# Two-block mixer kernel on one core: z products first in the first SSD group, and sixteen modulation tiles moved out of SSD groups 2 and 3 into attention and merge

## Chip, cores and metric

One core of one Trainium2 chip runs the whole program as one launch. The metric is the time of one execution in device microseconds (us): the median of the runs shown.

## What is computed

512 tokens of 1024 dimensions, all in f32, go through a first block and a second one. What the change touches lies in the first block:

```
mod = silu(c) @ w_ada + b_ada                  # 6 x 1024 numbers
shift1, scale1, gate1, shift2, scale2, gate2 = split(mod, 6)
h = rms_norm(x, norm1_w) * (1 + scale1) + shift1
q, k, v, xBC, z, dt_raw, gates = split(h @ w_in)
attn = softmax attention(q, k, v)              # 16 heads, 4 kv heads
ssd  = ssd_mixer(xBC, z, dt_raw)               # conv, 4 groups, both directions, * silu(z), norm
merged = sigmoid(g_attn) * (attn @ w_attn_out) + sigmoid(g_ssd) * (ssd @ w_ssd_out)
x = x + gate1 * (merged @ w_o)
h2 = rms_norm(x, norm2_w) * (1 + scale2) + shift2
x = x + gate2 * (relu(h2 @ w_mlp1)**2 @ w_mlp2)
```

The second block (a gated linear recurrence, then latent attention, then a norm) is untouched.

## The kernel before

Every product is made from f32 operands split in a high and a low part, so each 128x128 by 128x512 step is three matmuls (`mm3`, printed in the profile as lines L174, L175 and L176). A GEMM with eight contraction tiles is thus 24 matmuls on TensorE (PE). Its 512 KB weight tile is loaded by `weight()`: an SP-issued DMA (L159) into a slot of the pool `wr`, a cast on ScalarE (ACT) to the high part `wh` (L162), and a subtraction for the low part `wl` (L165) on VectorE (DVE) or GpSimd (POOL). `wr`, `wh` and `wl` have four slots each, so weights run up to four GEMMs ahead of PE. PSUM for GEMMs is the pool `pm`, also four slots: the fifth GEMM waits until the first one's reader is done.

The order of the program text is turned into one queue per engine by a scheduler: it pulls ready work from later in the text forward, and each engine then runs its own queue strictly in order.

**Modulation.** `mod` has 48 columns of 128. `mod_tiles(j)` (L274) makes one: a 512 KB tile `wada` of `w_ada` is loaded by a DMA on SP into a slot of the same pool `wr`, and one DVE instruction (L279) multiplies it by silu(c) and sums along the row into column j of `modc`. Columns 0 to 15 are made in norm1. Columns 16 to 23 are gate1, 24 to 31 shift2, 32 to 39 scale2, 40 to 47 gate2. All of 16 to 47 get their bias in one DVE instruction after merge (L373), and are first used after that. So the time at which these 32 are made is free, and the table `MODS` spreads the first sixteen of them over SSD groups 2 and 3 (six and ten), eight go into attention (letters "m" of the table `ATT`), and the last eight into merge, one for each of its eight steps.

**The SSD mixer** (`ssd`, `ssd_core`, `ssd_out`). norm1 hands over seven finished products: dt and the six xBC tiles of group 0. For these the program does the first half of `dt_product` (softplus, ending with `av`, L465), then convolutions (`conv`: ACT L498, four DVE steps L507, tanh L515, DVE L516). The second half of `dt_product` (L471 to L490: decay sums on PE, copies, exponentials) stands before the fourth convolution. Then each group g runs its `ssd_core`: transposes to token-major (L561, L566), the product CB (L572) with two masked copies (DVE L576), and the 18 steps of the table `CORE`: six state steps S (DVE L596 scales, PE L598, DVE L603 and L604, PE L608, DVE L612, L613 or L615), eight mixer steps M for one head each (PE L623, then four times ACT L629, DVE L631, ACT L633, DVE L635, then ACT L642 and the POOL product L643), four outputs Y for two heads each (PE L650 and L653, DVE L657, L659, L670, POOL L666). Y0 follows M3, Y3 is last and needs the POOL products of M6 and M7.

Between those steps `ssd` spreads fills, GEMMs that keep PE busy: the z products of the same group (one DVE instruction L534 as reader, used by L659), the xBC products of the next group with their convolutions (six DVE instructions each with the reader), and `ssd_out` of the group before. In group 0 the fills alternate between xBC and z:

```
fill = so + [xs[0], zs[0], xs[1], zs[1], xs[2], zs[2], xs[3], zs[3], xs[4], xs[5]]
```

**Attention** (`attention`) overlaps the scores, the softmax (DVE L755, L759, ACT L758, POOL L763), transposes and products of 16 heads with the qkv products, the stacks of rotated q and k (DVE L820 to L823 and L170, PE L807), and gate products.

**Merge** (`merge`) has eight steps of two GEMMs: a gate product (weights `w_gate`), the attention output (`w_attn_out`) with DVE readers L921 and L922, and `mod_tiles([40 + m])`. Merge's early work is pulled forward into the end of attention by the scheduler. After it come the bias of `modc` (L373), `gate_rows` and the output projection.

Of the kernel before, what the change touches and what calls it, by code (L numbers as in the profile page):

```python
# [18 lines left out]
FIRST = [-1, 4, 5, 0, 1, 2, 3]  # L19
# [20 lines left out]
AORD = "s0 s1 s2 s3 f0 t0 m0 t1 m1 t2 m2 t3 m3 f1".split()  # L40
CORE = "S0 S1 M0 S2 S3 M1 S4 S5 M2 M3 Y0 M4 M5 Y1 M6 M7 Y2 Y3"
NC = 19
MODS = [0, 0, 6, 10]
WP = 0
TP = 0
LO = {"start": 5, "ssd": 8, "attn": 2, "merge": 3, "mlp": 0, "rglru": 3, "mla_in": 6, "mla": 5}
# [13 lines left out]
class Build:  # L60
# [616 lines left out]
    def ssd(self, first):  # L677
        nc, a = self.nc, self.a
        self.csb = self.c([128, 512], "csb", F32R)
        self.tk1 = self.c([128, 4, 128], "tk1")  # L680
        self.tk2 = self.c([128, 4, 128], "tk2")
        self.dcy = self.c([128, 4, 64], "dcy")
        self.ssacc = self.c([128, 512], "ssacc", pool=self.stack[-2]["c"])
        self.xb = [[None] * 6 for _ in range(4)]
        self.zt, self.ssdT = {}, {}
        for i, ps in zip(FIRST, first):
            if i < 0:
                dt = self.dt_product(ps)
                next(dt)
                continue  # L690
            if i == FIRST[4]:
                next(dt)
            with self.fills():
                self.xb[0][i] = self.conv(i if i < 4 else 16 + 4 * (i - 4), ps)
        with self.fills():
            for i in range(6):
                if i not in FIRST:
                    self.xbc(0, i)
        self.qk = {}
        for g in range(4):  # L700
            so = [lambda mp=mp: self.ssd_out(g - 1, mp) for mp in range(4)] if g else []
            zs = [lambda j=j: self.z(g, j) for j in range(4)]
            if g < 3:
                xs = [lambda i=i: self.xbc(g + 1, i) for i in (4, 5, 0, 1, 2, 3)]
                fill = so + [xs[0], zs[0], xs[1], zs[1], xs[2], zs[2], xs[3], zs[3], xs[4], xs[5]]
            else:
                with self.fills():
                    self.attn_tables(self.stack[-2]["c"])
                q0 = self.qkv(0)
                fill = so + zs + [lambda: next(q0, None)] * Q0  # L710
            k0 = 16 + sum(MODS[:g])
            k1 = k0 + MODS[g]
            fill = [lambda f=f, i=i: (f(), self.mod_tiles([k0 + i] if k0 + i < k1 else [])) for i, f in enumerate(fill)]
            n = 0
            for step, _ in enumerate(self.ssd_core(g)):
                while n < len(fill) and n * NC <= (step + 1) * len(fill):
                    with self.fills():
                        fill[n]()
                    n += 1
            while n < len(fill):  # L720
                with self.fills():
                    fill[n]()
                n += 1
        for mp in range(4):
            with self.fills():
                for _ in range(2):
                    next(q0, None)
            self.ssd_out(3, mp)
        with self.fills():
            for _ in q0:  # L730
                pass
        R = self.ssacc
        p = self.ps()
        nc.tensor.matmul(p, lhsT=self.ones, rhs=self.ssacc, start=True, stop=True)
        nc.scalar.activation(out=R, in_=p, func=AF.Sqrt, scale=1.0 / 2048, bias=self.eps)
        nc.vector.reciprocal(out=R, in_=R)
# [100 lines left out]
    def attention(self):  # L837
        nc = self.nc

        def scores(h, t):  # L840
            stk, (kh, kl), vv = self.qk[h // 4]
            p = self.ps()
            s = slice(t * 128, t * 128 + 128)
            nc.tensor.matmul(p, lhsT=stk[h % 4][:, s], rhs=kh, start=True, stop=False)
            nc.tensor.matmul(p, lhsT=stk[h % 4][:, s], rhs=kl, start=False, stop=True)
            return self.softmax_tile(p, 512)

        def turn(pr, kt):
            p = self.ps()
            for t in range(NT):  # L850
                nc.tensor.transpose(out=p[:, t * 128:t * 128 + 128], in_=pr[t][:, kt * 128:kt * 128 + 128],  # L851
                                    identity=self.ident)
            ph, pl = self.t("ph", F32R), self.t("pl", F32R)
            self.split(ph, pl, p)
            return ph, pl

        def mix(h, po, kt, parts):
            vv, (ph, pl) = self.qk[h // 4][2], parts
            nc.tensor.matmul(po, lhsT=vv[:, kt], rhs=ph, start=kt == 0, stop=False)
            nc.tensor.matmul(po, lhsT=vv[:, kt], rhs=pl, start=False, stop=kt == 3)  # L860

        def output(h, po):

            if h % 2 == 0:
                self.of = self.t("of")
            of = self.of
            d = slice(64 * (h % 2), 64 * (h % 2) + 64)
            e = slice(64 * (1 - h % 2), 64 * (1 - h % 2) + 64)
            nc.scalar.copy(out=of[d], in_=po[e])
            nc.vector.tensor_tensor(out=of[d], in0=of[d], in1=po[d], op=ALU.add)  # L870
            if h % 2 == 1:
                self.split(self.oh[:, h // 2], self.ol[:, h // 2], of)

        gates = [lambda m=m: self.gate_ssd(m) for m in range(8)]
        mods = list(range(16 + sum(MODS), 40))

        def fill(what):
            with self.fills():
                for x in what:
                    if x == "q":  # L880
                        next(nxt, None)
                    elif x == "g" and gates:
                        gates.pop(0)()
                    elif x == "m" and mods:
                        self.mod_tiles([mods.pop(0)])

        pr = [scores(0, t) for t in range(NT)]
        for h in range(16):
            g, i = divmod(h, 4)
            if i == 0:  # L890
                nxt = self.qkv(g + 1) if g < 3 else iter(())
            last = pr
            if i == 3:
                fill("q" * 8)
            pr = []
            po = self.pm() if POM else self.ps()
            turned = {}
            for x in AORD:
                j = int(x[1])
                if x[0] == "s" and h < 15:  # L900
                    pr.append(scores(h + 1, j))
                elif x[0] == "t":
                    turned[j] = turn(last, j)
                elif x[0] == "m":
                    mix(h, po, j, turned.pop(j))
                elif x[0] == "f":
                    fill(ATT[g][2 * i + j])
            output(h, po)
        fill("g" * 8 + "m" * len(mods))

    def merge(self):
        nc, a = self.nc, self.a
        oh, ol, acc, mh, ml = self.oh, self.ol, self.accS, self.mh, self.ml
        for m in range(8):
# [7 lines left out]
                self.split(mh[:, m], ml[:, m], th)  # L922

            self.gemm_cm([[a["w_attn_out"][m]]], lambda k: (oh[:, k], ol[:, k]), evac)
            self.mod_tiles([40 + m])

    def gate_rows(self, j, s):
        nc, a = self.nc, self.a
# [598 lines left out]
```

## Time and profile before

| | us |
|---|---|
| median of 3 runs | 1647.56 (1647.04 to 1647.98) |
| the profiled execution | 1645.17 |
| its span on the core | 1643.4 |
| PE busy in the span | 1579.3 (96%) |
| DVE busy | 1126.8 (69%) |
| ACT busy | 789.5 (48%) |
| POOL busy | 446.5 (27%) |

The mean granted clock of TensorE was 0.995 of full speed. How to read it: PE is busy nearly all the time, so what counts is the few places where PE has a gap, and which engine ends that gap. A busy share of 69% for DVE is an average over stages in which it is full and stages in which it is half empty. In the trace SSD group 0 runs from about 94 to 178 us, group 1's core begins there, the fills of groups 2 and 3 with their modulation tiles lie between 239 and 451 us, attention ends about 742 us, merge about 812 us.

### The profile page before, as it was taken

Reading aid. Unit: us, or ns where it says so; the run is one execution under the profiler, and the core shown is the slowest. Engines: PE = TensorE matmul, PEld = TensorE weight load, DVE = VectorE, ACT = ScalarE, POOL = GpSimd, SP = SyncE. Lnnn points to the kernel's source line nnn. Section 1 sums busy time; section 2 is a strip of 40 time slices with the busy share of each in tenths; the row PEclk is TensorE's granted clock in tenths of the full one; section 3 lists DMA queues with packets and bytes.
Section 4 is the critical chain, followed back from the end, with each engine's and each line's share of the span. In section 5 each row is a group of like instructions: output and inputs, shape, how many; then the busy total and the mean of one; then the engine's idle time right before and its main releaser. Section 6 shows DMA issues by size and latency. Waiting matters only on the chain.

```text
span 1643.4 us, 20885 instructions
## 1 busy us (share of the span) xinstructions
PE 1579.3 (96%) x7696; PEld 1279.9 (78%) x7696; DVE 1126.8 (69%) x1948; ACT 789.5 (48%) x1517; POOL 446.5 (27%) x322
## 2 busy tenths in 40 slices
PE   5989999999999999999999999999999999999998
PEld 3767677677688778778889888888888778988886
DVE  6899689689869988874454344343458884747873
ACT  4347546355465667663344232322337662455652
POOL 3414345254252344321133011111141011321012
PEclk9999999999999999999999999999999999999999
DMA  7511124224222222215323232323323222322211
GB/s 255 197 57 60 52 87 130 66 82 146 78 77 91 71 71 90 78 52 192 103 64 116 90 103 91 102 90 103 112 70 99 87 90 67 100 69 71 64 62 52
DMA packets 50648, 153.54 MB, mean 93 GB/s; under 512 B 8177, under 2 KB 12913, under 8 KB 50546
## 3 DMA queue, kind: packets, MB, share of 16 engines
q1 hardware_dynamic: 50546, 152.22, 28.9%
q8 instruction: 60, 0.98, 0.2%
q14 instruction: 42, 0.34, 0.1%
HBM read 150.10 MB, written 2.10 MB: 93 GB/s over the span
## 4 chain that ended last, share of the span: by engine, by line
PE 72%; DVE 16%; ACT 4%; issue 3%; POOL 3%; DMA 1%; SPq 0%; DVEq 0%; POOLq 0%; ACTq 0%
PE pm L174 19%; PE pm L175 19%; PE pm L176 19%; DVE acc L507 2%; PE px L608 1%; DVE wada L279 1%; DVE nmax L755 1%; DVE wl L165 1%; PE px L851 1%; PE px L598 1%; POOL rs L254 1%; DVE w L635 1%; PE px L860 1%; PE px L653 1%; PE px L650 1%
## 5 line engine op out<-in xcount | busy, mean ns | idle before, releaser
L162 ACT CAST wh<-wr 128x1024 fp32r<-128x1024 f32 (+5 forms) x245 | 239.5, 980 | 390.3 <-PE pm L175 176.0
L165 DVE TENSOR_TENSOR wl<-wr,wh 128x1024 fp32r<-128x1024 f32 (+2 forms) x170 | 201.6, 1187 | 182.3 <-ACT wh L162 181.6
L165 POOL TENSOR_TENSOR wl<-wr,wh 128x1024 fp32r<-128x1024 f32 (+3 forms) x75 | 175.9, 2347 | 530.6 <-ACT wh L162 483.3
L174 PE MATMUL pm<-hh,wh 128*128 128x512 f32 (+1 forms) x432 | 172.9, 404 | 7.9 <-ACT hh L169 6.2
L175 PE MATMUL pm<-hl,wh 128*128 128x512 f32 (+1 forms) x432 | 175.0, 405 | 3.4 <-POOL hl L170 3.4
L176 PE MATMUL pm<-hh,wl 128*128 128x512 f32 (+1 forms) x432 | 172.4, 399 | 0.0
L986 POOL TENSOR_TENSOR r<-r 128x512 f32<-128x512 f32 x32 | 50.9, 1589 | 252.3 <-ACT r L985 252.3
L174 PE MATMUL pm<-h,wh 128*128 128x512 f32 (+1 forms) x288 | 105.4, 366 | 0.0
L175 PE MATMUL pm<-h,wh 128*128 128x512 f32 (+1 forms) x288 | 105.2, 365 | 0.0
L176 PE MATMUL pm<-h,wl 128*128 128x512 f32 (+1 forms) x288 | 105.2, 365 | 0.0
L174 PEld LDWEIGHTS pm<-hh,wh 128*128 128x128 f32 (+1 forms) x432 | 81.2, 188 | 29.4 <-ACT hh L169 7.6
L175 PEld LDWEIGHTS pm<-hl,wh 128*128 128x128 f32 (+1 forms) x432 | 81.6, 189 | 26.1 <-POOL hl L170 6.3
L174 PE MATMUL pm<-wh,rh 128*128 128x512 f32 x256 | 99.8, 390 | 0.0
L763 POOL TENSOR_SCALAR pr<-pr,psum 128x512 f32<-128x512 f32 x64 | 64.6, 1021 | 129.1 <-DVE psum L759 71.1
L176 PE MATMUL pm<-wh,rl 128*128 128x512 f32 x256 | 99.6, 389 | 0.0
L175 PE MATMUL pm<-wl,rh 128*128 128x512 f32 x256 | 99.6, 389 | 0.0
L176 PEld LDWEIGHTS pm<-hh,wl 128*128 128x128 f32 (+1 forms) x432 | 81.5, 189 | 19.7 <-issue 3.1
L507 DVE SCALAR_TENSOR_TENSOR acc<-pm,conv_w_s,acc 128x510 f32<-128x510 f32 (+2 forms) x114 | 84.5, 741 | 9.0 <-ACT acc L498 8.0
L643 POOL TENSOR_TENSOR e<-e,w 128x512 f32<-128x512 f32 x32 | 52.0, 1625 | 100.5 <-ACT e L642 74.5
L279 DVE SCALAR_TENSOR_TENSOR wada<-wada,cs 128x1024 f32<-128x1024 f32 x48 | 66.3, 1390 | 15.6 <-DMA wada<-in_w_ada 15.3
L758 ACT ACTIVATE pr<-px,nmax 128x512 f32<-128x512 f32 (+2 forms) x96 | 60.4, 637 | 29.9 <-DVE nmax L755 24.0
L174 PE MATMUL pm<-ha,wh 128*128 128x512 f32 (+1 forms) x192 | 68.2, 355 | 0.0
(401 smaller groups left out, 4130.1 us busy)
## 6 DMA issues: line engine op xcount, KB each, us to landing
wr<-in_w_mlp SPq DMA_DIRECT2D x64, 512.0 KB, 3.4
wada<-in_w_ada SPq DMA_DIRECT2D x48, 512.0 KB, 3.9
wr<-in_w_xbc SPq DMA_DIRECT2D x24, 512.0 KB, 3.5
wr<-in_w_in_a SPq DMA_DIRECT2D x20, 512.0 KB, 3.5
wr<-in_w_z SPq DMA_DIRECT2D x16, 512.0 KB, 3.5
wr<-in_w_ssd_out SPq DMA_DIRECT2D x16, 512.0 KB, 3.5
wr<-in_w_gate SPq DMA_DIRECT2D x16, 512.0 KB, 4.0
wr<-in_w_qkv SPq DMA_DIRECT2D x16, 384.0 KB, 3.1
```

What stands on the lines that cost most here:

```text
L162: nc.scalar.copy(out=hi[:, :n], in_=raw[:, :n])
L165: eng.tensor_tensor(out=lo[:, :n], in0=raw[:, :n], in1=r32(hi[:, :n]), op=ALU.subtract)
L174: m(out, lhsT=lh, rhs=rh, start=start, stop=False)
L175: m(out, lhsT=lh, rhs=rl, start=False, stop=False)
L176: m(out, lhsT=ll, rhs=rh, start=False, stop=stop)
L254: g.tensor_tensor(out=r, in0=r, in1=self.mhalf.to_broadcast(list(ss.shape)) if len(ss.shape) == 2 else self.mhalf.unsqueeze(2).to_broadcas ...
L279: nc.vector.scalar_tensor_tensor(out=w, in0=w, scalar=1.0, in1=self.cs, op0=ALU.mult, op1=ALU.mult, accum_out=self.modc[:, j:j + 1])
L507: nc.vector.scalar_tensor_tensor(out=acc[:, lo:hi], in0=ps[:, lo + o:hi + o], scalar=w[:, j:j + 1], in1=acc[:, lo:hi], op0=ALU.mult, op1=A ...
L643: self.e("ew").tensor_tensor(out=e, in0=e, in1=w, op=ALU.mult)
L758: nc.scalar.activation(out=e[:, :n], in_=p, func=AF.Exp, bias=nmax, accum_out=s)
L763: self.e("norm").tensor_scalar(out=e[:, :n], in0=e[:, :n], scalar1=s, scalar2=1.0, op0=ALU.mult, op1=ALU.mult)
L986: self.e("sq").tensor_tensor(out=r, in0=r, in1=r, op=ALU.mult)
```

## The change

Three things change in the text; no operation is added or left out, only its place moves.

- `MODS` becomes all zero: SSD groups 2 and 3 make no modulation columns. Attention's eight are now columns 16 to 23 (before 32 to 39). Each of merge's eight steps makes three columns (24+m, 32+m, 40+m) where it made one. So sixteen tiles, with sixteen DMAs on SP and sixteen DVE instructions, move from the SSD groups to merge's text.
- In group 0, z(0,0) and z(0,1) stand before the second half of `dt_product`, and this stands after all six convolutions where it stood before the fourth one.
- Group 0's fills are now z(0,2), z(0,3) and then the six xBC products of group 1.

```diff
-MODS = [0, 0, 6, 10]
+MODS = [0, 0, 0, 0]
...
-            if i == FIRST[4]:
-                next(dt)
             with self.fills():
                 self.xb[0][i] = self.conv(i if i < 4 else 16 + 4 * (i - 4), ps)
         with self.fills():
             for i in range(6):
                 if i not in FIRST:
                     self.xbc(0, i)
+            self.z(0, 0)
+            self.z(0, 1)
+        next(dt)
...
-                fill = so + [xs[0], zs[0], xs[1], zs[1], xs[2], zs[2], xs[3], zs[3], xs[4], xs[5]]
+                fill = zs[2:] + xs if g == 0 else so + [xs[0], zs[0], xs[1], zs[1], xs[2], zs[2], xs[3], zs[3], xs[4], xs[5]]
...
-        mods = list(range(16 + sum(MODS), 40))
+        mods = list(range(16, 24))
...
-            self.mod_tiles([40 + m])
+            self.mod_tiles([24 + m, 32 + m, 40 + m])
```

What this does to the queues, at the three places of which the prediction speaks (line numbers of the changed kernel are one higher after line 690):

DVE at the start of group 0's core, before. `acc` is a convolution, `zt` a z product, `cb` and `xw` the first tiles of the core; the convolutions here read the first and third fill of group 1's xBC tiles from `pm`.

```order
108 L507 SCALAR_TENSOR_TENSOR acc_758<-pm_727,conv_w_s,acc_758 128x510
109 L507 SCALAR_TENSOR_TENSOR acc_758<-pm_727,conv_w_s,acc_758 128x511 x2
110 L576 TENSOR_TENSOR cb_772<-px_767,k_tri_s 128x512
111 L507 SCALAR_TENSOR_TENSOR acc_758<-pm_727,conv_w_s,acc_758 128x510
112 L576 TENSOR_TENSOR cb_774<-px_767,k_tri_s 128x512
113 L596 TENSOR_TENSOR xw_777<-xtm_695,tk_587 128x512
114 L516 SCALAR_TENSOR_TENSOR th_764<-th_764,acc_758 128x512
115 L534 SCALAR_TENSOR_TENSOR zt_817<-zt_817,pm_786 128x512
116 L596 TENSOR_TENSOR xw_820<-xtm_695,tk_587 128x512
```

The same place of DVE in the changed kernel:

```order
109 L534 SCALAR_TENSOR_TENSOR zt_705<-zt_705,pm_674 128x512
110 L534 SCALAR_TENSOR_TENSOR zt_739<-zt_739,pm_708 128x512
111 L576 TENSOR_TENSOR cb_834<-px_829,k_tri_s 128x512
112 L534 SCALAR_TENSOR_TENSOR zt_826<-zt_826,pm_795 128x512
113 L576 TENSOR_TENSOR cb_836<-px_829,k_tri_s 128x512
114 L596 TENSOR_TENSOR xw_839<-xtm_763,tk_587 128x512
115 L534 SCALAR_TENSOR_TENSOR zt_888<-zt_888,pm_857 128x512
116 L596 TENSOR_TENSOR xw_848<-xtm_763,tk_587 128x512
117 L615 TENSOR_TENSOR yoff_838<-px_845,tk_587 128x512
118 L615 TENSOR_TENSOR yoff_838<-px_854,tk_587 128x512
119 L596 TENSOR_TENSOR xw_915<-xtm_763,tk_587 128x512
120 L631 SCALAR_TENSOR_TENSOR e_895<-pf_891,tk_586,e_895 128x128
```

The first four GEMMs are now z products with one reader each, and the convolutions of group 1's tiles come later.

POOL at the end of group 0, before (`e` is the product of a mixer step, `ssacc` the sum of squares, `wl` a weight's low part):

```order
44 L666 TENSOR_TENSOR ssacc<-ssacc,sq_1276 128x512
45 L643 TENSOR_TENSOR e_1287<-e_1287,w_1288 128x512
46 L165 TENSOR_TENSOR wl_1657<-wr_1655,wh_1656 128x1024
47 L643 TENSOR_TENSOR e_1351<-e_1351,w_1352 128x512
48 L666 TENSOR_TENSOR ssacc<-ssacc,sq_1387 128x512
```

The same place of POOL in the changed kernel:

```order
43 L165 TENSOR_TENSOR wl_1657<-wr_1655,wh_1656 128x1024
44 L643 TENSOR_TENSOR e_1240<-e_1240,w_1241 128x512
45 L666 TENSOR_TENSOR ssacc<-ssacc,sq_1276 128x512
46 L643 TENSOR_TENSOR e_1327<-e_1327,w_1328 128x512
47 L643 TENSOR_TENSOR e_1351<-e_1351,w_1352 128x512
```

The low part `wl_1657` stood between the products of M6 and M7; now it stands ahead of M5's.

DVE in the last quarter of attention, before (`wada` is the first of merge's modulation tiles, `pl`, `st`, `m`, `nmax` and `psum` belong to attention):

```order
931 L759 RECIPROCAL psum_6053<-psum_6053 128x1
932 L279 SCALAR_TENSOR_TENSOR wada_6930,modc<-wada_6930,cs 128x1024
933 L170 TENSOR_TENSOR pl_6098<-px_6092,ph_6097 128x512
934 L823 TENSOR_TENSOR m_6136<-m_6136,m_6137 128x256
935 L170 TENSOR_TENSOR pl_6109<-px_6103,ph_6108 128x512
```

The same place of DVE in the changed kernel:

```order
916 L760 RECIPROCAL psum_6005<-psum_6005 128x1
917 L279 SCALAR_TENSOR_TENSOR wada_6882,modc<-wada_6882,cs 128x1024
918 L170 TENSOR_TENSOR pl_6050<-px_6044,ph_6049 128x512
919 L824 TENSOR_TENSOR m_6088<-m_6088,m_6089 128x256
920 L170 TENSOR_TENSOR pl_6061<-px_6055,ph_6060 128x512
921 L170 TENSOR_TENSOR st_6095<-m_6088,st_6094 128x4x64
922 L165 TENSOR_TENSOR wl_6818<-wr_6816,wh_6817 128x1024
923 L170 TENSOR_TENSOR pl_6072<-px_6066,ph_6071 128x512
924 L279 SCALAR_TENSOR_TENSOR wada_6885,modc<-wada_6885,cs 128x1024
925 L170 TENSOR_TENSOR pl_6083<-px_6077,ph_6082 128x512
```

Where attention's last part held four of merge's modulation tiles (rows 932, 952, 983 and 1012 of DVE), it now holds twelve (from row 917 to row 1008); the other twelve stand in merge between rows 1043 and 1061.

## Rows read from the trace of the kernel before

**Rows 1.** The page: busy time of each engine, then TensorE's granted clock in slices.

```profile
PE 1579.3 (96%) x7696; PEld 1279.9 (78%) x7696; DVE 1126.8 (69%) x1948; ACT 789.5 (48%) x1517; POOL 446.5 (27%) x322
PEclk9999999999999999999999999999999999999999
```

**Rows 2.** By stage: length; busy PE, PEld, DVE, ACT, POOL; clock, DMA share, GB/s.

```profile
107.00:170.00 63.00, 62.52 (x289) 44.79 (x287) 61.35 (x123) 39.88 (x99) 24.66 (x13) 1.00 0.15 51
178.00:278.00 100.00, 97.19 (x445) 72.76 (x445) 80.17 (x139) 54.54 (x120) 40.37 (x20) 1.00 0.27 85
340.00:414.00 74.00, 71.58 (x362) 54.86 (x361) 69.20 (x122) 41.33 (x88) 35.88 (x17) 1.00 0.38 125
661.00:694.00 33.00, 29.41 (x153) 22.82 (x153) 30.81 (x63) 20.59 (x43) 11.83 (x9) 1.00 0.23 70
742.00:812.00 70.00, 70.00 (x309) 57.65 (x308) 32.32 (x43) 21.50 (x28) 7.56 (x3) 1.00 0.47 158
```

**Rows 3.** PE's timeline, group 0: start us, us, engine line op, [idle before <-releaser].

```profile
94.39 0.77 PE L471 MATMUL px<-av,k_tri_s 128*128 128x128 f32 x2 [3.28 <-issue]
...
106.48 0.47 PE L174 MATMUL pm<-hh,wh 128*128 128x512 f32 x1 [1.65 <-DVE acc L507]
```

**Rows 4.** DVE's timeline, start of group 0's core.

```profile
102.10 0.69 DVE L516 SCALAR_TENSOR_TENSOR th<-th,acc 128x512 f32<-128x512 f32 x1 [0.76 <-ACT th L515]
...
105.60 0.74 DVE L507 SCALAR_TENSOR_TENSOR acc<-pm,conv_w_s,acc 128x510 f32<-128x510 f32 x1
...
114.67 0.34 DVE L631 SCALAR_TENSOR_TENSOR e<-pf,tk,e 128x128 f32<-128x128 f32 x1
```

**Rows 5.** Timeline, end of group 0: DVE, POOL and PE.

```profile
166.26 0.34 DVE L635 SCALAR_TENSOR_TENSOR w<-cb,tk,w 128x128 f32<-128x128 f32 x1
...
166.65 2.40 POOL L165 TENSOR_TENSOR wl<-wr,wh 128x1024 fp32r<-128x1024 f32 x1 [2.35 <-DVE w L635]
...
169.00 1.72 POOL L643 TENSOR_TENSOR e<-e,w 128x512 f32<-128x512 f32 x1
...
170.78 0.43 PE L653 MATMUL px<-e,xtm 128*64 128x128 f32 x2 [1.26 <-POOL e L643]
```

**Rows 6.** What PE waited for between 178 and 394 us: total, times, longest.

```profile
PE px L608 <- DVE st L604: 6.9, 5, 2.5
```

**Rows 7.** Timeline of group 2, DVE beside POOL, and the PE wait after it.

```profile
328.54 2.79 POOL L165 TENSOR_TENSOR wl<-wr,wh 128x1024 fp32r<-128x1024 f32 x1 [12.19 <-DVE w L635]
329.02 2.85 DVE L516 SCALAR_TENSOR_TENSOR th<-th,acc 128x512 f32<-128x512 f32 x1
...
334.83 1.12 PE L608 MATMUL px<-st,th 128*128 128x512 f32 x2 [1.84 <-DVE st L604]
```

**Rows 8.** What PE waited for between 390 and 440 us: total, times, longest.

```profile
PE px L598 <- DVE xw L596: 2.6, 2, 1.4
PE px L561 <- DVE th L516: 1.1, 1, 1.1
```

**Rows 9.** DVE's timeline, one of the modulation tiles among group 3's work.

```profile
389.52 1.21 DVE L279 SCALAR_TENSOR_TENSOR wada<-wada,cs 128x1024 f32<-128x1024 f32 x1
```

**Rows 10.** What PE waited for between 640 and 742 us: total, times, longest.

```profile
PE px L807 <- DVE st L170: 1.7, 2, 1.4
```

**Rows 11.** DVE's timeline in merge.

```profile
770.42 1.23 DVE L279 SCALAR_TENSOR_TENSOR wada<-wada,cs 128x1024 f32<-128x1024 f32 x1 [8.63 <-DMA wada<-in_w_ada]
...
784.19 0.18 DVE L373 TENSOR_TENSOR modc<-modc,b_ada_s 128x32 f32<-128x32 f32 x1
```

**Rows 12.** Groups of instructions, whole run: xcount, busy us, mean ns, idle before.

```profile
L279 DVE SCALAR_TENSOR_TENSOR wada<-wada,cs 128x1024 f32<-128x1024 f32 x48 | 66.3, 1390 | 15.6 <-DMA wada<-in_w_ada 15.3
```

**Rows 13.** The page's DMA issues: xcount, KB each, us to landing.

```profile
wada<-in_w_ada SPq DMA_DIRECT2D x48, 512.0 KB, 3.9
```

## The prediction

> **What bounds the kernel now.** I read the page first. PE is busy 96% of the span and DVE 69%, and the granted clock stands at nine tenths or more throughout [rows 1]. So a change can win only where PE has a gap; a shorter or longer DVE queue counts only through such a gap. The busy time by stage comes next [rows 2]: in group 0 DVE is as full as PE (61.35 and 62.52 of 63 us), in group 3 nearly so (69.20 of 74), in one stretch of late attention it is fuller than PE (30.81 against 29.41 of 33), and in merge PE has no gap at all (70.00 of 70) while DVE is busy for 32.32. Then I looked in the lists of waits and the timeline for what ends each gap: in group 0 a wait for a PSUM slot [rows 3] and one for a POOL product [rows 5], in group 2 state steps that wait for DVE [rows 6, 7], in group 3 the next core's first tiles, also from DVE [rows 8], in late attention the rotated keys from DVE [rows 10]. Every gap of these stages is thus ended by DVE or POOL.
>
> The sum is made against the profiled execution: 1645.17 us, a span of 1643.4 and 1.77 around it. The median of the runs is 1647.56, that is 2.39 more; I add this at the end. No change means within 0.2% of the median here, 3.3 us either way, which is about what a measurement of this kernel can tell from none.
>
> **Part 1: the PSUM slot of group 0.** Before, four GEMMs fill `pm` and the fifth waits until the last of four convolution steps on the first is done: 105.60 + 0.74 = 106.34, and PE starts at 106.48 after 1.65 us idle [rows 3, 4], so it had arrived at 104.83. In the changed queue the first GEMM is a z product with a single reader, the instruction right behind the L516 of 102.10 [rows 4]. What stands ahead of it on DVE is the same work, so it ends near 102.10 + 0.69 + 0.7 = 103.5, before 104.83. The gap goes: **-1.65**.
>
> **Part 2: the DVE queue of group 0.** From `av` to the last L635 of M7 the queue holds exactly the same instructions (25 L507, 7 L516, 4 L534, 64 of the mixer and so on), only in another order, so only idle time can differ. Before, convolutions stood between the first state steps and covered the way from L596 over PE, ACT and PE to L615. Now L615 follows almost at once. By the rows, from the end of the first L596 (107.53) to its L615 (110.81) it takes 3.3 us, of which two short instructions now cover 1.2; the same way for the second costs about one more, less the 0.76 and 0.52 that DVE idles now: I take **2.2 us** of extra idle. M7's last L635 then ends near 166.60 + 2.2 = 168.8 instead of 166.60 [rows 5].
>
> What is late next is the POOL product of M7 and PE's Y3. But POOL's queue also changes: the low part that ran from 166.65 to 169.00 ahead of that product [rows 5] now stands ahead of M5's. So the product can start at about 169.0, as it does now, and Y3 starts near 170.8, as now. PE has the same instructions up to group 1's first state step, so the 1.65 won is waited for again at Y3: the sum of parts 1 and 2 is **0**. Ends: -1.65 - 1.26 = **-2.9**, if DVE catches up (less idle than 2.2), and **+1.8**, if the idle is 4.0 instead, no gap row being longer than 3.28 [rows 3].
>
> The decay sums are given later in the text, but their first matmul (L471) waits for `av` after 3.28 us of idle [rows 3], and both `av` and L471 have the same place in their queues as before. Nothing won or lost. The loads on SP are the same ten, z first; none is waited for here.
>
> **Part 3: sixteen modulation tiles leave groups 2 and 3.** Each is one DVE instruction of 1.39 us on average over all 48 [rows 12], 1.21 where it stands alone [rows 9]. Group 2's six lie between 239 and 284 us, where PE has no gap and DVE has room (80.17 of 100 just before 278, [rows 2]): **0**. The waits of 6.9 us for L604 [rows 6] stay: one lies in group 1, which had none of these tiles, and the others come from DVE instructions that are long beside POOL, such as L516 with 2.85 us beside a low part of 2.79, ahead of a PE wait of 1.84 [rows 7].
>
> Group 3's ten lie between 350 and 451. Where PE waits 1.1 us for the last convolution and 2.6 for two L596 [rows 8], DVE had done several of them just ahead, one at 389.52 [rows 9]; two before the first wait make 2.4 us, more than it, and two more stand before the second. So the first, and the longest of the two others (1.4), go: 1.06 + 1.35 = **-2.4**. Ends: 0, if the freed time goes to the tables of attention and to `ssd_out`, which stand in the same queue, and -3.7 with the third wait of 1.2.
>
> **Part 4: late attention.** Merge's tiles are pulled forward there: twelve instead of four. Eight more instructions of 1.21 are 9.7 us of DVE. Some five of them, 6.1 us, fall into the full stretch 661 to 694 [rows 2], ahead of the rotated keys for which PE waits there already [rows 10]. The cover is PE's own queue: 30 more matmuls of gate and output GEMMs now stand ahead of the last stack (L807), and with 70.00 us for 309 matmuls in merge [rows 2] these are 30 x 0.227 = 6.8 us. They are missing in merge later, so nothing is paid twice. On DVE nothing else is lost, but softmax, the copies of transposed scores and evictions are queued behind a tile that has not landed. All 48 waited 15.3 us in total for their DMA [rows 12], 8.63 of these in one place in merge [rows 11]; the other 6.7 over 47 tiles are 0.14 each. Twelve of these in a row, issued in threes by SP through the same four slots, wait longer than one at a time: I take **+1.5**, about ten times 0.14. Ends: -1.0, if the filler is more than needed, and +8.6, if a wait like that in merge falls here.
>
> **Part 5: merge.** Twelve tiles instead of four: eight more times 1.22 are 9.8 us on a DVE that is busy for 32.32 of 70 [rows 2]. The moving of SP's loads: eight more of 512 KB in 70 us add 60 GB/s to 158. A tile lands 3.9 us after its issue [rows 13]; a weight is loaded up to four GEMMs, 4 x 5.45 = 21.8 us, ahead of its use, so a weight that stands behind three tiles in SP's queue still comes in time. The bias L373 runs at 784.19 [rows 11]; even 9.8 later, and with another wait of 8.63, it is done by 803, ahead of the end of merge at 812 where its columns are first read. **0**; without that cover, the end is one tile's landing, +3.9.
>
> **The sum.** 0 - 2.4 + 1.5 + 0 = -0.9 us: 1644.3 for the profiled execution, and with 2.39 added **1646.7 us**.
>
> A word on the neighbour of these tiles. Rows show that a DVE instruction with two inputs in SBUF becomes long beside POOL: 2.85 us for L516 against 0.69 alone [rows 4, 7]. The Trainium skill, page "SBUF — State Buffer", section "Who interferes with whom", says that such an instruction shares a port pair with GpSimd, as an exclusive lock under which the loser blocks. The modulation product is of this kind. By that rule each of the five tiles moved into the full stretch of attention, where POOL is busy 11.83 of 33 us, would pay up to the 1.6 us that separate the extremes of rows for such an instruction, and the page speaks against the move; the trace agrees for L516, and says nothing of attention's tiles yet.
>
> **The rivals.**
>
> *Everything gained is kept.* DVE catches up in group 0 (-2.9), group 3 loses all three waits (-3.7), and attention costs nothing: -6.6, so 1647.56 - 6.6 = **1641.0 us**. For it: DVE's work is the same in group 0, and ten tiles leave a full stretch. Against: the way from L596 to L615 must be waited for somewhere, and attention's stretch is full. Chance 0.22.
>
> *A landing in attention.* DVE stops at a tile whose DMA could not start, because its slot in `wr` still holds a weight that waits for its cast, and the softmax behind it stops with it. Place: the second or third tile of a triple between 667 and 719 us. Price: the wait of 8.63 seen in merge [rows 11] in place of my 1.5. It decides once a wait is longer than the filler in front of PE's next attention instruction, some 2 us. -2.4 + 8.6 = +6.2: **1653.8 us**, slower. For it: three tiles in a row need three of four slots. Against: the four tiles that stand in attention's end now did not wait. Chance 0.17.
>
> *Group 0 pays more.* DVE's idle is 4.0 and Y3 comes 1.8 later: -2.4 + 1.5 + 1.8 = +0.9, **1648.5 us**, no change. Chance 0.13.
>
> **How the numbers follow.** My forecast has 0.48. Its own range, 1643.5 to 1650, sticks out a little on the lower side (0.05) and hardly on the upper (0.03). Faster: 0.22 + 0.05 = 0.27. Slower: 0.17 + 0.03 = 0.20. No change: 0.40 + 0.13 = 0.53. The range that leaves out 2 in 10 goes from the first rival's 1641.0 to 1653.0, just short of the second one's.
>
> **What would show it.** Right: no PE gap near 106 us; a Y3 that starts between 170 and 171.5 and waits for POOL about 3 us; no wait of L561 near 394 and one L598 wait at most; waits of L604 about 7 us in total as before; PE without gap in merge. Wrong: a DVE wait of over 2 us for `wada` between 660 and 742, or a weight cast in merge that waits for its DMA and PE after it.

## The result, and the profile after

The change makes the kernel slower: 1656.44 us median of 4 runs (1656.08 to 1657.19) against 1647.31 (1647.04 to 1647.98), a ratio of 1.0055 with a 95% interval of 1.0038 to 1.0073. That is 9.1 us, where 1646.7 was forecast, and outside the range that was predicted.

The profiled execution has a span of 1654.4 us, 11.0 more than before. Where they arise is read by setting the same PE instructions of the two traces against each other. The first decay sum (L471) starts at 93.61 us (94.39 before), the first state step of group 1 (L598) at 191.71 (182.66), the first `gate_rows` matmul after merge at 823.29 (812.23); from there on the two traces take the same (831.13 and 831.15). So group 0 loses 9.8 us between L471 and group 1, and the way from there to the end of merge 2.0; L471 itself comes 0.8 earlier.

The page's first line: PE works 6.5 us more for the same matmuls than before [rows 1], DVE 4.6 less.

```profile
PE 1585.8 (96%) x7696; PEld 1282.3 (78%) x7696; DVE 1122.2 (68%) x1948; ACT 789.0 (48%) x1517; POOL 433.9 (26%) x322
```

Busy time by stage after the change (from:to, length, then PE, PEld, DVE, ACT, POOL, clock, DMA share, GB/s): group 0 without its first microseconds, group 3, the full stretch of late attention, and merge. They answer to [rows 2]; the later ones are moved by 9 to 11 us, about what the kernel is late there.

```profile
107.00:180.00 73.00, 66.39 (x291) 45.78 (x289) 68.14 (x128) 39.51 (x96) 25.86 (x14) 0.95 0.16 51
349.00:423.00 74.00, 73.54 (x368) 55.94 (x368) 58.48 (x108) 43.74 (x92) 30.26 (x17) 1.00 0.22 68
671.00:705.00 34.00, 30.33 (x154) 23.64 (x153) 33.01 (x64) 18.84 (x40) 10.64 (x9) 1.00 0.39 119
753.00:823.00 70.00, 69.97 (x314) 57.05 (x313) 44.42 (x64) 24.28 (x33) 7.20 (x3) 1.00 0.64 211
```

Group 3 has become what was wanted: DVE falls from 69.20 to 58.48 of 74 us, PE rises from 71.58 to 73.54. Merge takes 12.1 us more of DVE (44.42 for 32.32) without a PE gap. In group 0 PE is not full any more (66.39 of 73), and DVE is fuller than PE (68.14).

The timeline of group 0 after the change shows what DVE does there:

```profile
102.86 0.43 DVE L490 TENSOR_TENSOR tk<-tk,tk 128x256 f32<-128x256 f32 x1 [2.97 <-ACT tk L489]
...
107.89 2.37 POOL L165 TENSOR_TENSOR wl<-wr,wh 128x1024 fp32r<-128x1024 f32 x1 [15.66 <-ACT wh L162]
107.95 2.85 DVE L596 TENSOR_TENSOR xw<-xtm,tk 128x512 f32<-128x512 f32 x1
...
113.89 0.69 DVE L615 TENSOR_TENSOR yoff<-px,tk 128x512 f32<-128x512 f32 x1 [1.89 <-PE px L608]
116.55 0.69 DVE L615 TENSOR_TENSOR yoff<-px,tk 128x512 f32<-128x512 f32 x1 [1.97 <-PE px L608]
...
125.89 2.39 POOL L165 TENSOR_TENSOR wl<-wr,wh 128x1024 fp32r<-128x1024 f32 x1 [3.08 <-ACT wh L162]
126.33 2.50 DVE L596 TENSOR_TENSOR xw<-xtm,tk 128x512 f32<-128x512 f32 x1
...
175.45 0.34 DVE L635 SCALAR_TENSOR_TENSOR w<-cb,tk,w 128x128 f32<-128x128 f32 x1
...
176.32 1.28 POOL L643 TENSOR_TENSOR e<-e,w 128x512 f32<-128x512 f32 x1 [1.21 <-ACT e L642]
...
178.98 0.43 PE L653 MATMUL px<-e,xtm 128*64 128x128 f32 x2
```

Three things are to be seen. DVE waits 2.97 us for ACT's exponential, and nearly 2 us for each of the first two L615. Two L596 take 2.85 and 2.50 us, each beside a low part on POOL. (Not each such meeting lengthens DVE: beside the next low part, at 135.91, two L596 take 0.69 and 0.75, and it is POOL's instruction that takes 3.31.) And POOL's last product follows M7 closely: it starts 0.53 us after the last L635, where before it waited behind a low part [rows 5], and ends 1.8 us after it instead of 4.1. But the DVE queue ends at 175.79 instead of 166.60, and of the 2.3 us won on POOL only 1.0 reaches Y3: PE comes to Y3 1.4 us after the product is done, straight from other work, and no longer waits for POOL there.

I measure this queue in each run from the start of `av` (L465) to the end of M7's last L635, 138 instructions, and split it: idle time; lengthening, the sum of what each instruction takes above the lower quartile of the same instruction and shape in the whole run, where that is over 0.15 us; and the rest. Before: 72.7 us = 3.9 idle + 4.3 lengthened + 64.5. After: 82.7 = 9.7 + 8.3 + 64.7. The work is the same, as the order said; idle time grew by 5.8 and lengthening by 4.0. The two L596 alone make 4.0 of the 8.3. In each of the sixteen traces of this document, every instruction of this queue that counts as lengthened overlaps an instruction of POOL.

The granted clock is the third part. The two longest stretches at half clock (1.2 GHz) after the change, then two late ones:

```profile
92.42:99.24 6.82, 5.63 (x15) 4.67 (x16) 5.51 (x13) 2.15 (x5) 0.00 (x0) 0.50 0.27 77
167.51:174.34 6.83, 5.98 (x16) 3.93 (x16) 6.83 (x18) 6.08 (x20) 2.12 (x3) 0.50 0.19 70
232.36:235.78 3.42, 3.42 (x6) 1.58 (x5) 1.23 (x3) 0.00 (x0) 0.00 (x0) 0.50 0.00 0
505.43:508.84 3.41, 3.41 (x9) 2.67 (x8) 2.87 (x7) 1.94 (x4) 1.28 (x1) 0.50 0.00 0
```

Before, the same clock lasted for 3.4 us at 94.35 and 3.4 at 172.86, and nowhere else between 60 and 1640 us:

```profile
94.35:97.77 3.42, 3.38 (x10) 2.94 (x11) 2.11 (x6) 2.15 (x5) 0.00 (x0) 0.50 0.34 131
172.86:176.27 3.41, 3.41 (x12) 2.39 (x12) 1.11 (x3) 2.09 (x4) 0.00 (x0) 0.50 0.00 0
```

The first stretch begins in both kernels within the idle 3.3 us ahead of L471. The second lies at the end of the core: after the change it begins within a wait of 3.0 us ahead of L174 (167.95), before it 2.1 us behind the wait at Y3. Half of 13.7 - 6.8 us is 3.4 us of PE's work that group 0 may have lost so, and as much later.

### The profile page after: what moved, and what is told of

Its sections match the earlier page's. It is cut to its first block, busy times and chain, and to the rows that moved or that the text cites. A ratio compares the mean times of both kernels' runs of the same rounds, so it can differ in the third digit from the quotient of the medians.

```text
span 1654.4 us, 20886 instructions
## 1 busy us (share of the span) xinstructions
PE 1585.8 (96%) x7696; PEld 1282.3 (78%) x7696; DVE 1122.2 (68%) x1948; ACT 789.0 (48%) x1517; POOL 433.9 (26%) x322
## 4 chain that ended last, share of the span: by engine, by line
PE 73%; DVE 16%; ACT 4%; issue 4%; POOL 2%; DMA 1%; SPq 0%; DVEq 0%; POOLq 0%; ACTq 0%
PE pm L175 19%; PE pm L174 19%; PE pm L176 19%; DVE acc L507 2%; DVE wada L279 1%; DVE wl L165 1%; DVE nmax L756 1%; PE px L608 1%; PE px L852 1%; PE px L653 1%; PE px L650 1%; PE px L598 1%; POOL rs L254 1%; PE px L174 1%; PE px L175 1%
## 5 line engine op out<-in xcount | busy, mean ns | idle before, releaser
L165 POOL TENSOR_TENSOR wl<-wr,wh 128x1024 fp32r<-128x1024 f32 (+3 forms) x75 | 170.1, 2269 | 549.0 <-ACT wh L162 502.2
L174 PE MATMUL pm<-hh,wh 128*128 128x512 f32 (+1 forms) x432 | 173.0, 404 | 7.2 <-ACT hh L169 7.1
L174 PE MATMUL pm<-h,wh 128*128 128x512 f32 (+1 forms) x288 | 105.4, 366 | 0.0
L174 PEld LDWEIGHTS pm<-hh,wh 128*128 128x128 f32 (+1 forms) x432 | 81.3, 189 | 29.1 <-ACT hh L169 8.2
L174 PE MATMUL pm<-wh,rh 128*128 128x512 f32 x256 | 99.8, 390 | 0.0
L643 POOL TENSOR_TENSOR e<-e,w 128x512 f32<-128x512 f32 x32 | 49.4, 1544 | 85.0 <-ACT e L642 82.8
L174 PE MATMUL pm<-ha,wh 128*128 128x512 f32 (+1 forms) x192 | 68.2, 355 | 0.0
```

The costliest lines, as they stand in the source:

```text
L165: eng.tensor_tensor(out=lo[:, :n], in0=raw[:, :n], in1=r32(hi[:, :n]), op=ALU.subtract)
L174: m(out, lhsT=lh, rhs=rh, start=start, stop=False)
L643: self.e("ew").tensor_tensor(out=e, in0=e, in1=w, op=ALU.mult)
```

## The experiments

Each is a kernel of its own, compared with the kernel before on the same chip in five rounds. Not all experiments ran on the same chip, so where two of them are compared below, it is by what each differs from the kernel before beside it. The table gives median, ratio with its interval, and the DVE queue of group 0 in the profiled execution (138 instructions; in e12 141, three convolution steps more).

| run | us | ratio to before | queue = idle + lengthened + rest |
|---|---|---|---|
| before, after | | 1, 1.0055 | 72.7 = 3.9+4.3+64.5, 82.7 = 9.7+8.3+64.7 |
| e1 group 0 part only | 1657.72 | 1.0074 (1.0061-1.0087) | 81.7 = 8.7+8.7+64.3 |
| e2 tiles only | 1644.25 | 0.9990 (0.9982-0.9999) | 72.7 = 4.0+4.2+64.6 |
| e3 z first, sums early | 1655.03 | 1.0054 (1.0042-1.0066) | 79.5 = 5.3+10.0+64.2 |
| e4 sums late only | 1652.38 | 1.0038 (1.0025-1.0050) | 76.4 = 6.9+5.0+64.5 |
| e5 two z ahead, then alternate | 1657.55 | 1.0073 (1.0060-1.0086) | 81.9 = 8.0+9.2+64.7 |
| e6 as e3, no low parts on POOL | 1651.46 | 1.0034 (1.0021-1.0047) | 79.6 = 8.0+6.9+64.7 |
| e7 before, no low parts on POOL | 1641.96 | 0.9982 (0.9974-0.9991) | 72.4 = 3.6+4.3+64.5 |
| e8 tiles only, PE kept busy | 1650.25 | 1.0028 (1.0017-1.0039) | 81.2 = 5.5+9.5+66.2 |
| e9 before, no POOL work | 1641.45 | 0.9966 (0.9955-0.9977) | 72.1 = 5.3+2.7+64.1 |
| e10 as e1, no POOL work | 1644.27 | 0.9989 (0.9980-0.9998) | 74.9 = 9.3+2.0+63.7 |
| e11 tiles of group 3 only | 1644.04 | 0.9982 (0.9973-0.9992) | 72.7 = 3.9+4.5+64.3 |
| e12 xBC first, tiles moved | 1649.57 | 1.0015 (1.0006-1.0024) | 79.4 = 6.2+7.0+66.2 (141) |
| e13 before, no L643 and L666 | 1645.09 | 0.9996 (0.9986-1.0005) | 72.0 = 5.6+2.3+64.1 |
| e14 as e1, no L643 and L666 | 1654.94 | 1.0053 (1.0040-1.0066) | 79.9 = 10.0+6.2+63.7 |

**e1 and e2: the two halves of the change.** e1 keeps MODS, attention and merge as before; e2 keeps group 0 as before.

```diff
 e1, to the changed kernel:
-MODS = [0, 0, 0, 0]
+MODS = [0, 0, 6, 10]
...
-            self.mod_tiles([24 + m, 32 + m, 40 + m])
+            self.mod_tiles([40 + m])
 e2, to the kernel before:
-MODS = [0, 0, 6, 10]
+MODS = [0, 0, 0, 0]
...
-            self.mod_tiles([40 + m])
+            self.mod_tiles([24 + m, 32 + m, 40 + m])
```

> Only the group 0 part of the change (z first, decay sums late); the sixteen modulation tiles stay in groups 2 and 3. Theory A (nearly all of the loss is made in group 0): +9 us against before, the first L598 of group 1 at about 191.7 us instead of 182.7, and half-clock stretches near 92 to 99 and 167 to 174 us. Rival B (the moved modulation tiles lose it through merge and attention): about 0 to +2.

> Only the modulation tiles are moved, group 0 as before. Theory A: +2 us or less against before, with the waits of L561 and L598 near 394 and 409 us shorter and attention's end a little longer. Rival B: +8 us or more.

Theory A holds in where the loss is made: +12 us and -1.6 us add up to the measured change within the intervals, and L598 of group 1 starts at 191.00 in e1. The size was +9, and one sign missed: with the same DVE order as the changed kernel, e1 has no stretch at half clock near 94 us but one of 3.4 at 109.07, and still loses 9.1 us between L471 and group 1, where the changed kernel loses 9.8. Its DVE waits from 94 to 165 us begin with these:

```profile
DVE yoff L615 <- PE px L608: 5.5, 2, 3.5
DVE cb L576 <- PE px L572: 0.9, 1, 0.9
DVE tk L490 <- ACT tk L489: 0.9, 1, 0.9
```

In this execution 2.1 us more are lost between group 1 and the end; one stretch at half clock at 231.95 is worth up to 1.7 of them, the remainder stays open. In e2 the lists of what PE waited for, 390 to 440 us and then 640 to 742, are these, in the same stretches as [rows 8, 10]:

```profile
PE px L598 <- DVE xw L596: 1.0, 2, 0.8
PE pm L175 <- DVE yl L670: 0.3, 1, 0.3
```

```profile
PE px L860 <- DVE pl L170: 2.4, 3, 1.5
PE px L844 <- DVE of L870: 1.3, 1, 1.3
PE px L807 <- DVE st L170: 0.4, 1, 0.4
```

Group 3's 3.7 us have become 1.3, which is 2.4 less. But a wait that was not there before stands at group 2's first state step: 0.8 us for L596 (L598, 291.01 us; in the changed kernel 303.35). Over 190 to 520 us PE's waits thus fall from 12.4 to 10.8, by 1.6 as the time does. Attention's end had 1.7 for L807 [rows 10] and, before,

```profile
PE px L844 <- DVE of L870: 1.3, 1, 1.3
PE px L860 <- DVE pl L170: 1.1, 3, 0.5
```

so 4.1 in all, and has 4.1 again. One tile waits 0.5 us for its DMA there.

**e3 and e4: the two halves of the group 0 part.** In e3 the sums stand where they stood, in e4 alone they stand late:

```diff
 e3, to the changed group 0:
+            if i == FIRST[4]:
+                next(dt)
...
-        next(dt)
 e4, to the kernel before:
-            if i == FIRST[4]:
-                next(dt)
...
+        next(dt)
         self.qk = {}
```

> The group 0 part with the decay sums back before the fourth convolution, z first kept, modulation tiles as before. Theory C (the late decay sums make the loss: eleven GEMM matmuls stand ahead of L481 where seven did, ACT's L482 and L489 and DVE's L490 run late and the whole core starts late): about +2 against before, half-clock stretch near 94 us no longer than before. Rival D (z first makes it: DVE, which bounds the core, has no convolutions to do while it waits for the first state steps and pays for them later): +5 to +8.

> Only the decay sums late; fills alternate between xBC and z as before, modulation tiles as before. Theory C: +4 to +6 against before. Rival D: 0 to +2. If the sum of this run and of z first with early sums falls short of the whole group 0 part by several us, the two work together, through the clock for example.

Both cost, z first more (9 us) than late sums (6.5), and together 12, less than their sum. So neither theory holds alone: C expected about +2 for e3, D at most +2 for e4 and at most +8 for e3. Theory C was right on the way of the late sums: with late sums eleven GEMM matmuls stand ahead of L481 where seven did, though L471 keeps its place, and in e4's list of DVE waits between 94 and 170 us the first two are the exponential behind it and the state steps:

```profile
DVE tk L490 <- ACT tk L489: 2.0, 1, 2.0
DVE yoff L615 <- PE px L608: 1.6, 2, 1.0
```

The profiled execution of e4 (1648.55) was the fastest of its runs, so its queue, 3.7 us longer than before, shows rather less than the median.

**e5 and e12: other orders of the fills.**

```diff
 e5, to e3:
-                fill = zs[2:] + xs if g == 0 else ...
+                fill = [xs[0], zs[2], xs[1], zs[3]] + xs[2:] if g == 0 else ...
 e12, to e2, for g == 0:
-                [xs[0], zs[0], xs[1], zs[1], xs[2], zs[2], xs[3], zs[3], xs[4], xs[5]]
+                [xs[0], xs[1], zs[0], xs[2], zs[1], xs[3], zs[2], xs[4], zs[3], xs[5]]
```

> z(0,0) and z(0,1) ahead, decay sums early, but the eight fills alternate between xBC and z instead of the two remaining z first; tiles as before. If the loss of z first comes from DVE, which has no convolutions to do early and pays for them later, about half of the 9 us comes back (+4 to +6 against before). If it comes from the first two z products alone, nothing comes back (+9).

> The opposite order in group 0: two xBC products ahead of the first z, then alternating; tiles moved as in tiles only. If convolutions early in the core are what covers DVE's waits, DVE idles no longer than before in group 0 and the time is that of tiles only (-1.6 against before) within 2 us. If the order before is just the one with the fewest meetings of DVE and POOL, the lengthened part of group 0 grows as in all other orders and it is 3 us or more slower than tiles only.

Both are misses for the idea that early convolutions are what matters. e5 brings the convolutions forward and is no faster than e3 (12 us over the kernel before, where e3 had 9; the intervals overlap slightly); e12 puts them further forward than before and is 4 us slower than tiles only, as its second alternative had it. In both, idle time and lengthening are larger than in the kernel before.

**e6, e7, e9, e10, e13, e14: POOL's part.** In group 0 these leave out POOL's low parts of weights (the high part is used twice), or its products L643 and sums L666, or all of it, each in an old and a new order; the computation is changed by that, the set of DVE's instructions is not. DVE's order in group 0 is exactly that of the kernel before in e7, e9 and e13, and that of e1 in e10 and e14; only e6's differs from its counterpart e3, at 43 of 138 places. Leaving out the low parts does one thing more: in e6, e7, e9 and e10 the queue starts some 4 us earlier (89.3 to 89.8 us) and PE's 3.3 us of idle ahead of L471 are gone. Both runs of a pair have that, so only differences within a pair are used.

```diff
 low parts:
+        if self.nolo and eng is nc.gpsimd:
+            return v[1], v[1]
 products and sums:
-            self.e("ew").tensor_tensor(out=e, in0=e, in1=w, op=ALU.mult)
+            if g:
+                self.e("ew").tensor_tensor(out=e, in0=e, in1=w, op=ALU.mult)
```

> z first with early decay sums, and POOL makes no low parts of weights in group 0: the GEMMs whose low part POOL would make use the high part twice, so the output is not the reference's. Theory E (in the z-first order POOL's low parts meet DVE instructions with both inputs in SBUF, L596, L603 and L516, which take 2.3 to 2.9 us instead of 0.7): 4 us or more faster than z first with them, so +3 to +5 against before, and these DVE instructions at 0.7 us. If POOL has no part in it: +8 or more, as z first.

> The kernel before with the same left out in group 0 (POOL's low parts; the high part is used twice, so the output is not the reference's). It is the measure for the run above: -1 to -2 against before, since there the low parts mostly run beside convolutions, which read PSUM and keep their 0.74 us, and only the one at 166.65 us stands ahead of Y3.

> The kernel before without POOL's work of group 0: no low parts of weights (the high part is used twice), no product with w (L643), no sum of squares (L666), so the output is not the reference's. DVE's queue is the same. If the lengthened DVE instructions of group 0 come from POOL, they are gone: from av to M7's last L635 it takes 72.7 - 4.3 = 68.4 us.

> The group 0 part of the change (z first, sums late) with the same work of POOL left out. Theory F (two causes, DVE's idle time and meetings with POOL): from av to M7's last L635 it takes 81.7 - 8.7 = 73.0 us, 4 to 5 us more than the kernel before without POOL, and the loss against that kernel is about half of the 12 us. If the meetings are only a consequence and idle time takes their place: 78 us or more and a loss as large as with POOL. If the meetings are all: 69 us and no loss.

> The kernel before without POOL's products L643 and sums L666 of group 0, low parts kept (the output is not the reference's). Reference for the next run: -1 to -3 against before.

> The group 0 part of the change (z first, sums late) with the same left out. If the products L643 make the new order expensive, 2 to 4 us more than the kernel before without them, as when all of POOL's work is gone. If it is the low parts that meet state steps (L596 took 2.5 to 2.9 us twice), these stay long and the loss is 8 us or more.

DVE's groups of instructions L596 and L635 in group 0 (count, busy us, mean ns; from 94 to 165 us, in e6 from 89 to 170, so that 24 or all 32 of L635 are in it) in e1, with all of POOL's work:

```profile
L635 DVE SCALAR_TENSOR_TENSOR w<-cb,tk,w 128x128 f32<-128x128 f32 x24 | 9.8, 408 | 0.0
L596 DVE TENSOR_TENSOR xw<-xtm,tk 128x512 f32<-128x512 f32 x6 | 8.1, 1354 | 0.0
```

In e14, with low parts but without L643:

```profile
L596 DVE TENSOR_TENSOR xw<-xtm,tk 128x512 f32<-128x512 f32 x6 | 8.4, 1406 | 0.0
L635 DVE SCALAR_TENSOR_TENSOR w<-cb,tk,w 128x128 f32<-128x128 f32 x24 | 8.2, 343 | 0.0
```

In e6, with L643 but without low parts (the lines are three higher there):

```profile
L638 DVE SCALAR_TENSOR_TENSOR w<-cb,tk,w 128x128 f32<-128x128 f32 x32 | 14.8, 462 | 0.0
L599 DVE TENSOR_TENSOR xw<-xtm,tk 128x512 f32<-128x512 f32 x6 | 4.1, 686 | 0.0
```

In e10, without either (lines three higher too):

```profile
L638 DVE SCALAR_TENSOR_TENSOR w<-cb,tk,w 128x128 f32<-128x128 f32 x32 | 10.9, 342 | 0.0
L599 DVE TENSOR_TENSOR xw<-xtm,tk 128x512 f32<-128x512 f32 x6 | 4.1, 685 | 0.0
```

So in the new order L596 is long because of the low parts and L635 because of the products, each alone. By time, the new order costs 12 us with all of POOL's work (e1), 9.9 without the products (e14 less e13), 9.5 without the low parts (e6 less e7, there with early sums, where e3 lost 9 with them), and 2.8 without both (e10 less e9). Theory F had half of the loss left; it is a quarter. The split of the queue says why, in the three pairs of the same two orders (e1 and before, e14 and e13, e10 and e9): idle time grows by 4.8, 4.4 and 4.0 us, with or without POOL, and lengthening by 4.4, 3.9 and -0.7. The idle time comes with the order, the lengthening with POOL's work. The clock does not explain what differs between the pairs: in each of them, and in e6 and e7, the new order has 3.4 us more at half clock in group 0 than the old. Theory F's figures for the queue missed (72.1 and 74.9 us where 68.4 and 73.0 were expected), since idle time rose where lengthening went, and low parts of weights that group 1 uses still ran on POOL beside it (in e9 from 128 and from 151 us). The expectation for e6, that the low parts alone make z first expensive, fell: leaving them out takes as much from the kernel before (3.6 us, where 1 to 2 were expected; its queue starts 4.1 us earlier). e13 without the products gains nothing clear of noise, where 1 to 3 us were expected; e14 keeps its loss, as its second alternative had it. What the low parts and the products each add when both are there isn't settled; either one is enough to keep most of the loss, for the products alone with the proviso that e6 has early sums and an order of its own.

**e8: the clock ahead of L471.** Ten matmuls on a finished tile, in the tiles-only kernel, fill PE's wait for `av` (the profile counts each f32 matmul twice, so x20):

```diff
+        warm = self.ps((128, 4, 64))
+        for _ in range(10):
+            nc.tensor.matmul(warm, lhsT=self.ones, rhs=sp[0], start=True, stop=True)
```

> The tiles-only kernel with ten extra matmuls of 256 columns, whose result nobody reads, in the 3.3 us in which PE waits for av ahead of L471. If the half clock of 94 to 97.4 us follows from that idle time, it is gone, and the time is 1 to 2 us below tiles only (-3 against before). If the clock falls all the same, the time is that of tiles only or a little above.

They do what was wanted to the clock. PE's timeline and the stretch behind it:

```profile
89.95 4.55 PE L467 MATMUL px<-sp,ones 128*128 128x256 f32 x20 [1.89 <-DVE sp L347]
```

```profile
94.00:97.50 3.50, 3.41 (x23) 2.81 (x22) 3.29 (x8) 2.43 (x5) 0.41 (x1) 1.00 0.00 0
```

The clock stays at full speed through 94 to 97.5 us, and the transposes L481 start 2.2 us earlier than before, with four GEMM matmuls ahead of them instead of seven. The other runs bear it out in the main: in the eleven that leave PE idle for 3.3 us or more ahead of L471, nine have a stretch at half clock that begins between 92.4 and 94.4 us, and in e1 and e14 it begins at 109.1 and 108.5; in the five that don't (e6 to e10) none begins between 60 and 157 us. Yet the kernel is 6 us slower than tiles only: with the matmuls in the text DVE's order differs at 68 of 138 places, and its queue takes 81.2 us. What PE wins here is lost on DVE behind it.

**e11: fewer tiles moved, and faster than before and after.** Only group 3's ten tiles are moved, group 2 keeps its six.

```diff
-MODS = [0, 0, 6, 10]
+MODS = [0, 0, 6, 0]
...
-        mods = list(range(16 + sum(MODS), 40))
+        mods = list(range(22, 30))
...
-            self.mod_tiles([40 + m])
+            self.mod_tiles([j for j in (30 + m, 38 + m) if j < 48] + ([46 + m] if m < 2 else []))
```

> Tiles moved out of group 3 alone: MODS is 0, 0, 6, 0, attention makes columns 22 to 29 and merge the other eighteen; group 0 as before. If the gain of moving tiles is made in group 3 and given back in attention's end, this is as fast as the tiles-only kernel or up to 1 us faster: -1.5 to -3 against before.

It is 0.18% faster than before (interval 0.08% to 0.27%), as expected. Against e2 the intervals overlap, so it is not shown whether moving group 2's six tiles as well wins or loses anything.

## Why the prediction was wrong

**Part 1 was right**, and so small that it didn't matter. The wait for a PSUM slot at 106.48 is gone; in its place PE waits 1.86 us for L596 at 110.95.

**Part 2 is the step that failed**, with "I take 2.2 us of extra idle" and, before it, "only in another order, so only idle time can differ". It measured 5.8 us more idle and 4.0 us more lengthening, and parts 1 and 2 together cost 9.8 us in group 0 where their sum was 0. (The terms that are written there give 3.3 - 1.2 + 1 - 0.76 - 0.52 = 1.8, not 2.2; that is a slip of no weight.) Two things were missing in it, and a third was nearly right.

- The late sums were costed at nothing because `av` and L471 keep their places. What moved is L481, four matmuls further back: eleven matmuls, most of them at half clock, run from 95.10 us until it starts at 99.75. ACT's copy of the sums waits for L481, its exponential stands behind that copy, and DVE's L490 and all that follows wait for the exponential: 2.97 us. I had followed a moved step to its first instruction only. Not all of this wait is the order's. In e1, with the same order and the clock full there, it is 0.9, and the two L615 wait 5.5 us instead of 3.9, right behind the half clock that comes later in that run. In e10, with no half clock near either, the two are 3.9 and 0.9. So some 1.5 to 2 us of the idle time go with the half clock, wherever it falls.
- The two L615 wait 1.89 and 1.97 us, 3.9 where I took some 3.1 before subtracting; this was nearly right by itself.
- The lengthening I costed at nothing, although [rows 7] showed L516 at 2.85 us beside POOL and I wrote of the rule only for attention's tiles. The Trainium skill, page "SBUF — State Buffer", section "Who interferes with whom", says that a DVE instruction with two inputs in SBUF contends with a GpSimd instruction that reads SBUF, and one with at most one such input, outside the two-port modes that it lists apart, does not. The trace agrees on both: L596 takes 2.85 us beside a low part and 0.685 without POOL's work, while convolutions, with one input in PSUM, have a mean of 0.74 us in group 0 of before, after, e3 and e4, and none of the whole kernel before takes over 0.752, though 15 of the 24 between 94 and 176 us that read a slot of `pm` run beside POOL. Beside the first two low parts of group 0 (103.75 and 124.40 us) the old order has only convolutions and other steps that read PSUM; the new one has an L596 in both places (107.89 and 125.89).

**Y3** came out as argued on POOL: its product no longer waits behind a low part. But it starts 8.2 us later (178.98 for 170.78) on a queue that ends 9.2 later, so only 1.0 of that gain is in the result; and the sign "waits for POOL about 3 us" did not come, since PE arrives after the product.

**The clock** had no term. Group 0 had 13.7 us at half instead of 6.8, worth up to 3.4 us of PE's work. It is not the main part of the loss: e1 has 3.4 us less of it than the changed kernel and loses 9.1 us in group 0 all the same. The two late stretches, as much again, are not shown to be the change's: such stretches stand behind group 0 in runs with the old order of group 0 too (e2 at 493.18, e11 at 335.87), and in executions of the kernel before the mean granted clock varies from 0.991 to 0.997 without any edit.

**Part 3 was right in size for group 3**: 2.4 us of waits went there, in e2 as in the changed kernel. Group 2, taken as 0, gained a wait of 0.8. **Part 4** was too dear: attention's end costs about 0 where I took 1.5. PE waits 1.3 us more for L860's input and 1.2 to 1.3 less for L807's, and none of merge's tiles there waits over 0.5 us for its DMA. **Part 5** held: PE has 69.97 of 70 us in merge, though DVE does 12.1 us more there and not 9.8.

Of the rivals, *group 0 pays more* named the right place and half of the mechanism (idle time, not lengthening) with a price of 1.8 where 9.8 was due. *Everything gained is kept* and *a landing in attention* did not happen. The bound of 1.8 rested on the longest gap seen before; but a queue that is as full as DVE's there sums every wait and every lengthening on it, and no single gap bounds that sum.

## What to carry to other kernels

Where an engine is full through a stage, an equal set of instructions in another order isn't an equal time: add up along that engine's queue what each instruction then waits for, and what POOL runs at that moment. An order in which instructions that read PSUM stand beside POOL's long ones is worth keeping: here every other order of group 0 that was tried (e1, e3, e4, e5, e8, e12) took 4 to 12 us more than the old one with the same tiles. Follow a moved step through every engine to the last one that waits for it, and move independent work (here the tiles) on its own, for a part that wins can hide in a whole that loses.

## What was not expected of the hardware

A wait of PE can be followed by a second loss: the 3.3 us ahead of L471 were followed by 3.4 us at 1.2 GHz before the change and 6.8 after it, and with ten matmuls in that wait the clock stayed at full speed (1.00 from 94 to 97.5 us). It isn't certain: in e1 and e14 the same wait was followed by full clock until 108 us. POOL's two kinds of work lengthened different DVE instructions (L596 from 0.69 to 1.4 us in the mean, L635 from 0.34 to 0.46). With low parts alone the new order still cost 9.9 us more than the old, with products alone (and early sums) 9.5, with neither 2.8.
